# Two matmuls for three in a seven-product matmul scheme on one Trainium2 core

## The chip, the cores and the metric

The kernel runs on 1 core of one Trainium2 chip. The time is device microseconds of one execution of the whole program, as the median of the runs shown. TensorE (PE) multiplies, VectorE (DVE) and ScalarE (ACT) work on SBUF and PSUM, GpSimd (POOL) works on SBUF and issues the accumulating DMAs, SyncE (SP) issues the others.

## What is computed

A two-layer decoder trunk on 512 tokens of width 2048, all in float32. Cut to what matters here:

```python
def _stick_breaking_mixer(x, k, v, w_q, w_out):
    q, g = _split(x @ w_q, (ATTN_W, ATTN_W))
    ...
    return (o * jax.nn.silu(g)) @ w_out

def reference(x, p, positions, w_in_a, w_out_a, w_q_b, w_kv_b, w_out_b, ...):
    ...
        x = _layer_norm(DN_ALPHA * x + y, ln_g[i], ln_b[i])
        x = x + (p[i] @ w_ple[i]) * jax.nn.sigmoid(x @ w_ple_gate[i])
        if i == N_A_LAYERS - 1:
            kb, vb = _split(x @ w_kv_b, (ATTN_W, ATTN_W))
    ...
```

The change touches the projections `x @ w_kv_b` and `x @ w_q` of the second layer: keys, values, queries and gates of 16 heads, each a product of a 128-column block of weights (2048 x 128) with the 512 tokens.

## The kernel before

Everywhere in the kernel a float32 product is made of float32r parts: an operand is split into a high part (its float32r rounding, by ACT) and a low part (the rest, by DVE), and three matmuls are summed: high by high, low by high and high by low. The order of work is one list of `Chunk`s, each with the weights of one 128 x 1024 tile `raw`. `run` goes through the list; at chunk c `plan` has placed steps for later chunks: the split of the weights of chunk c + 2 into `wh` (ACT, L299) and `wl` (DVE, L300), loads six chunks ahead, and the weight sums below. Every engine works its instructions in the order in which they were issued, and the splits come ahead of what a chunk's own end issues.

**The seven products.** `quads` (L194) works off 30 pairs of weight blocks. For a pair, blocks c1 and c2 are cut into row halves, the 2048 x 512 input into four quarters, and seven products P1 to P7 of sums of these give both 128 x 512 results (a Strassen-Winograd scheme). A product has one 128 x 1024 weight tile and one table of 8 input tiles `f` from `F` ("A11", "S1" and so on). Each `f` is 128 x 512: its first 256 columns (`HALF`) are the high part of 256 columns of input, its last 256 the low part (`split_halves`, L105). `form` (L856) hands the two halves out, and `multiply` (L186) runs 8 times three matmuls of 256 columns into the first half of a PSUM bank (L192).

**Banks and ends.** Bank E takes P7 and then P4, bank B takes P2, and bank A takes P1, P6, P5 and P3 in turn; a product that follows in the same bank adds to it, so intermediate values must be read out before the next one starts there. After P7, P1 and P6 ACT copies 256 columns of the bank to SBUF (`after7`, `after1`, `after6`); after P2, P5 and P4 DVE adds a copy and a bank, 128 x 256 (`after2` L237, `after5` L241, `after4` L245); after P3 ACT copies (`after3` L251). Then `b_done` takes a result over: for keys and queries a split, for gates a sigmoid and a product.

**Weight sums.** The tile of P6 is the sum of those of P7 and P1, and the tile of P4 of those of P6 and P2 (DVE, L292). The tiles of P7 and P5 get c2's half added by an accumulating DMA from POOL's queue (`add_load`, L287): that of P5 lands on the tile of P1 after P1's splits and P6's sum have read it, two chunks before P1 begins.

**Order of the pairs.** A pair's list is P7, P1, P3 of the pair before, P6, P2, P4, P5; the first pair starts with P1, P7, and the last P3 stands alone at the end. Attention of the heads is woven in: `b_att` (score matmuls, then ACT sigmoids, POOL masks, DVE scans) after P2 and P4 of the pair that follows a pair with a key block (15 of the 30 pairs, the last one among them), `b_tail` after P1 and P6 of the next (after the last P3 for the last head), and `b_values` (transposes) after P5 of the pair that has a value block. After the last pair's products `us_ahead` splits eight tiles `u` for the output projection `mix_out`.

```python
                product(q, "P3", "S4", "A", False, True, after3, fresh=(1, q["c"][1]))
...
            product(q, "P6", "S2", "A", False, False, after6, grown=q["P7"], plus=q["P1"])
            product(q, "P2", "A12", "B", True, True, after2, fresh=(1, c1))
            product(q, "P4", "A22", "E", False, True, after4, grown=q["P6"], plus=q["P2"])
            product(q, "P5", "S1", "A", False, False, after5, add=(0, c2), grown=q["P1"])
        third(qs[-1])
```

Of the kernel before, what the change touches and what calls it, by code (L numbers as in the profile page):

```python
# [10 lines left out]
OP = mybir.AluOpType  # L11
# [5 lines left out]
KT = D // P  # L17
# [14 lines left out]
HALF = T // 2  # L32
# [41 lines left out]
class Kernel:  # L74
# [109 lines left out]
            self.chunks.append(Chunk(loads, mms))  # L184

    def multiply(self, ch, ps, xs, start, stop):  # L186
        nc = self.nc
        for j in range(KT // 2):
            wh, wl = (z[:, j * P:(j + 1) * P] for z in (ch.h, ch.l))
            xh, xl = xs(j)  # L190
            for n, (a, b) in enumerate(((wh, xh), (wl, xh), (wh, xl))):
                nc.tensor.matmul(ps[:, :HALF], a, b, start=start and j == 0 and n == 0,  # L192
                                 stop=stop and j == KT // 2 - 1 and n == 2, skip_group_check=True)

    def quads(self, sources, forms, done):

        nc = self.nc
        seq = []

        def product(q, name, form, acc, start, stop, after, fresh=None, add=None, grown=None, plus=None):  # L200
            def run(ch):
                if start:
                    q[acc] = self.ps("g")
                self.multiply(ch, q[acc], lambda j: forms(form, j), start, stop)
                after(q)
                ch.h = ch.l = None

            def rows(half, block):
                view, c = block
                return view[:, half::2, c:c + P]  # L210

            def loads(raw):
                nc.sync.dma_start(raw.rearrange("p (k c) -> p k c", k=8), rows(*fresh))

            ch = Chunk(loads if fresh else None, [])
            ch.product = run
            ch.grown = grown
            ch.add = rows(*add) if add else None
            ch.plus = plus
            q[name] = ch  # L220
            seq.append(ch)

        def after7(q):
            q.setdefault("s17", None) or q.__setitem__("s17", self.tt(s="s17"))
            nc.scalar.copy(q["s17"][:, HALF:], q["E"][:, :HALF])

        def after1(q):
            q.setdefault("s17", None) or q.__setitem__("s17", self.tt(s="s17"))
            nc.scalar.copy(q["s17"][:, :HALF], q["A"][:, :HALF])

        def after6(q):
            q["o2"] = self.tt(s="o2")
            nc.scalar.copy(q["o2"][:, :HALF], q["A"][:, :HALF])

        def after2(q):
            q["o1"] = self.tt(s="o1")
            nc.vector.tensor_tensor(q["o1"][:, :HALF], q["s17"][:, :HALF], q["B"][:, :HALF], op=OP.add)  # L237
            q["B"] = None

        def after5(q):  # L240
            nc.vector.tensor_tensor(q["o2"][:, HALF:], q["s17"][:, HALF:], q["A"][:, :HALF], op=OP.add)  # L241
            q["s17"] = None

        def after4(q):
            nc.vector.tensor_tensor(q["o1"][:, HALF:], q["o2"][:, :HALF], q["E"][:, :HALF], op=OP.add)  # L245
            q["E"] = None
            done(q["n"], 0, q["o1"])
            q["o1"] = None

        def after3(q):  # L250
            nc.scalar.copy(q["o2"][:, :HALF], q["A"][:, :HALF])  # L251
            q["A"] = None
            done(q["n"], 1, q["o2"])
            q["o2"] = None

        qs = [dict(n=n, c=c) for n, c in enumerate(sources)]
        for n, q in enumerate(qs):
            c1, c2 = q["c"]
            last = qs[n - 1] if n else None

            def third(q):
                product(q, "P3", "S4", "A", False, True, after3, fresh=(1, q["c"][1]))

            if not last:
                product(q, "P1", "A11", "A", True, False, after1, fresh=(0, c1))
            product(q, "P7", "S3", "E", True, False, after7, fresh=(1, c2), add=(0, c2))
            if last:
                product(q, "P1", "A11", "A", True, False, after1, fresh=(0, c1))
                third(last)
            product(q, "P6", "S2", "A", False, False, after6, grown=q["P7"], plus=q["P1"])  # L270
            product(q, "P2", "A12", "B", True, True, after2, fresh=(1, c1))
            product(q, "P4", "A22", "E", False, True, after4, grown=q["P6"], plus=q["P2"])
            product(q, "P5", "S1", "A", False, False, after5, add=(0, c2), grown=q["P1"])
        third(qs[-1])
        self.chunks += seq
        return qs
# [110 lines left out]
def _emit(k, x, p, positions, w_in, w_out_a, w_q, w_kv, w_out_b, ln_g, ln_b, w_ple, w_gate, freq, out):  # L387
    nc, const = k.nc, k.const
# [201 lines left out]
    xs = lambda m: xT[m]  # L590
# [252 lines left out]
    F = {}  # L843
# [11 lines left out]
        k.split_halves(f24, ((j, F["S2"]), (j, F["S4"])))  # L855

    def form(name, j):
        f = F[name][j]
        return f[:, :HALF], f[:, HALF:]

    def ln_apply(layer, ms):
        for m in ms:
# [203 lines left out]
    qs = k.quads([(where_b[a](ha), where_b[b](hb)) for a, ha, b, hb in plan_b], form, b_done)  # L1066
    for n, (a, ha, b, hb) in enumerate(plan_b):
        if a == "v":
            qs[n]["P5"].then(lambda h=ha: b_values(h))
        if a != "k":  # L1070
            continue
        qs[n + 1]["P2"].then(lambda h=ha: b_att(h, 0, 1))
# [4 lines left out]
    last = qs[-1]  # L1077
# [58 lines left out]
```

## Time and profile before

| what | value |
|---|---|
| median of 3 runs | 2148.35 us (2148.02 to 2149.95) |
| profiled execution, its own time | 2148.99 us |
| its span in the trace | 2147.3 us |
| PE busy | 2120.2 us, 99% of the span |
| PE weight loads busy | 1876.8 us, 87% |
| DVE busy | 1354.8 us, 63% |
| ACT busy | 967.9 us, 45% |
| POOL busy | 262.9 us, 12% |
| mean granted clock of PE | 0.996 |

The pairs of the seven-product scheme take 1056 to 1752 us of the span. A busy share tells how long an engine had an instruction in it; matmuls overlap each other, so what one costs is read from the distance of the starts of neighbours and not from its duration. A wait in the trace is idle time of an engine with the instruction that ended it. The profiled execution's own time is 0.64 us above the median, and 1.7 us above its span for what lies around it.

### The profile page before, as it was taken

What the parts mean: (1) busy time and instruction counts of PE and PEld (TensorE: products, weight loads), DVE (VectorE), ACT (ScalarE), POOL (GpSimd) and SP (SyncE); (2) the same over time, 40 slices, a digit from 0 to 9 for tenths busy, and PEclk for the clock granted to TensorE, in tenths of its full rate; (3) what the DMA queues carried; (4) which work ended last, traced back from release to release, by engine and by line L of the source; (5) the groups of instructions that cost most, each with busy time, mean ns of one, the idle gap of its engine ahead of it and who ended that gap; (6) DMA issues with size and microseconds to landing.
All of it is one profiled execution on the core that took longest, in us unless ns stands there. A gap on an engine that the chain in (4) does not pass through costs nothing.

```text
span 2147.3 us, 30976 instructions
## 1 busy us (share of the span) xinstructions
PE 2120.2 (99%) x12289; PEld 1876.8 (87%) x12289; DVE 1354.8 (63%) x2063; ACT 967.9 (45%) x1529; POOL 262.9 (12%) x287
## 2 busy tenths in 40 slices
PE   8999999999999999999999999999999989999999
PEld 7987888888888887888899999999999988887887
DVE  3576976566566547635778777777777765447432
ACT  3564345455453226423555455455555443226422
POOL 6111010000000100000022122121221111110000
PEclk9999999999999999999999999999999999999999
DMA  7332332222222232333567777778768863332341
GB/s 220 109 89 79 98 99 78 71 79 69 79 89 89 90 107 79 128 118 121 115 134 134 148 141 142 149 144 150 155 124 150 176 178 115 118 118 74 103 122 55
DMA packets 368800, 248.72 MB, mean 116 GB/s; under 512 B 13648, under 2 KB 354704, under 8 KB 368656
## 3 DMA queue, kind: packets, MB, share of 16 engines
q1 hardware_dynamic: 306256, 215.29, 34.9%
q0 software_dynamic: 62400, 31.46, 11.8%
q8 instruction: 96, 1.57, 0.3%
q14 instruction: 48, 0.39, 0.1%
HBM read 234.65 MB, written 12.06 MB: 115 GB/s over the span
## 4 chain that ended last, share of the span: by engine, by line
PE 92%; DVE 3%; issue 3%; ACT 1%; POOL 1%; DMA 0%; SPq 0%; POOLq 0%; DVEq 0%; ACTq 0%
PE g L192 25%; PE g L118 19%; PE g L119 19%; PE g L120 19%; PE s L611 2%; PE o L119 1%; PE o L120 1%; PE o L118 1%; PE s L118 1%; PE s L119 1%; PE s L120 1%; DVE wl L300 1%; PE s L545 1%; DVE z L866 1%; DVE z L865 0%
## 5 line engine op out<-in xcount | busy, mean ns | idle before, releaser
L300 DVE TENSOR_TENSOR wl<-raw,wh 128x1024 fp32r<-128x1024 f32 x452 | 555.8, 1234 | 389.7 <-ACT wh L299 386.4
L118 PE MATMUL g<-h,wh 128*128 128x512 f32 (+1 forms) x1808 | 704.4, 390 | 3.3 <-ACT h L102 3.3
L119 PE MATMUL g<-l,wh 128*128 128x512 f32 (+1 forms) x1808 | 698.9, 387 | 3.2 <-DVE l L103 3.2
L120 PE MATMUL g<-h,wl 128*128 128x512 f32 (+1 forms) x1808 | 698.5, 386 | 0.5 <-DVE wl L300 0.5
L192 PE MATMUL g<-f,wh 128*128 128x256 f32 x3360 | 621.6, 284 | 5.6 <-DVE o L241 5.6
L299 ACT CAST wh<-raw 128x1024 fp32r<-128x1024 f32 x452 | 473.0, 1051 | 335.6 <-PE g L119 223.7
L192 PEld LDWEIGHTS g<-f,wh 128*128 128x128 f32 x3360 | 530.5, 192 | 6.6 <-issue 5.8
L192 PE MATMUL g<-f,wl 128*128 128x256 f32 x1680 | 476.6, 284 | 1.9 <-DVE wl L300 1.9
L118 PEld LDWEIGHTS g<-h,wh 128*128 128x128 f32 x1808 | 340.1, 188 | 73.9 <-ACT h L102 4.8
L119 PEld LDWEIGHTS g<-l,wh 128*128 128x128 f32 x1808 | 340.4, 188 | 69.3 <-DVE l L103 4.8
L120 PEld LDWEIGHTS g<-h,wl 128*128 128x128 f32 x1808 | 340.2, 188 | 67.1 <-DVE wl L300 1.0
L192 PEld LDWEIGHTS g<-f,wl 128*128 128x128 f32 x1680 | 323.2, 192 | 3.5 <-DVE wl L300 2.7
L287 POOL DMA_DIRECT2D raw<-in_w_q_b_dram x60 | 94.4, 1894 | 571.9 <-issue 244.4
L103 DVE TENSOR_TENSOR l<-s,h 128x512 fp32r<-128x512 f32 (+1 forms) x128 | 73.0, 618 | 47.2 <-ACT h L102 47.2
L488 POOL TENSOR_TENSOR rb<-rb,sin 128x512 f32<-128x512 f32 (+2 forms) x29 | 36.0, 1241 | 475.3 <-ACT rb L486 320.2
L669 ACT ACTIVATE pr<-pr,s 128x128 f32<-128x128 f32 (+1 forms) x64 | 36.1, 563 | 126.1 <-DVE s L668 125.8
L102 ACT CAST h<-s 128x512 fp32r<-128x512 f32 (+1 forms) x128 | 61.1, 540 | 62.1 <-PE s L448 33.2
L815 POOL TENSOR_TENSOR a<-a,sq 128x512 f32<-128x512 f32 x30 | 40.3, 1343 | 342.1 <-ACT sq L813 341.9
L292 DVE TENSOR_TENSOR raw<-raw,raw 128x1024 f32<-128x1024 f32 x60 | 73.1, 1219 | 0.0
L684 DVE TENSOR_TENSOR_SCAN r<-keep,zeros 128x127 f32<-128x127 f32 (+1 forms) x64 | 54.4, 849 | 13.0 <-POOL keep L681 13.0
L489 DVE TENSOR_TENSOR ra<-ra,cos 128x512 f32<-128x512 f32 (+2 forms) x29 | 32.8, 1131 | 37.6 <-ACT ra L487 37.6
L813 ACT ACTIVATE sq<-z 128x512 f32<-128x512 f32 x30 | 19.0, 634 | 81.6 <-DVE z L806 81.6
(183 smaller groups left out, 1956.0 us busy)
## 6 DMA issues: line engine op xcount, KB each, us to landing
raw<-in_w_in_a_dram SPq DMA_DIRECT2D x132, 256.0 KB, 3.3
raw<-in_w_ple_gate_dram SPq DMA_DIRECT2D x64, 512.0 KB, 3.7
raw<-in_w_kv_b_dram SPq DMA_DIRECT2D x64, 512.0 KB, 6.4
raw<-in_w_q_b_dram SPq DMA_DIRECT2D x64, 512.0 KB, 6.9
raw<-in_w_q_b_dram POOLq DMA_DIRECT2D x60, 512.0 KB, 10.3
raw<-in_w_in_a_dram SPq DMA_DIRECT2D x32, 512.0 KB, 4.0
raw<-in_w_out_a_dram SPq DMA_DIRECT2D x32, 512.0 KB, 3.5
raw<-in_w_out_b_dram SPq DMA_DIRECT2D x32, 512.0 KB, 3.6
```

The lines of the kernel that those rows point to most:

```text
L102: nc.scalar.copy(h[:, lo:w], src[:, lo:w])
L103: nc.vector.tensor_tensor(l[:, lo:w], src[:, lo:w], h.bitcast(F32)[:, lo:w], op=OP.subtract)
L118: nc.tensor.matmul(out, ah, bh, start=start, stop=False)
L119: nc.tensor.matmul(out, ah, bl, start=False, stop=False)
L120: nc.tensor.matmul(out, al, bh, start=False, stop=stop)
L192: nc.tensor.matmul(ps[:, :HALF], a, b, start=start and j == 0 and n == 0, stop=stop and j == KT // 2 - 1 and n == 2, skip_group_check=True)
L287: self.nc.gpsimd.dma_start(ch.raw.rearrange("p (k c) -> p k c", k=8), ch.add, accum_op=OP.add)
L292: self.nc.vector.tensor_tensor(ch.raw, ch.raw, ch.plus.raw, op=OP.add)
L299: nc.scalar.copy(ch.h, ch.raw)
L300: nc.vector.tensor_tensor(ch.l, ch.raw, ch.h.bitcast(F32), op=OP.subtract)
L611: nc.tensor.transpose(banks[b][:, off + (i - j) * P:off + (i - j + 1) * P], a["p"][i][:, j * P:(j + 1) * P], ident)
L684: nc.vector.tensor_tensor_scan(r[:, 0:n - 1][:, ::-1], keep[:, 1:n][:, ::-1], zeros.to_broadcast([P, n - 1]), 1.0, op0=OP.mult, op1=OP.add)
```

## The change

In `multiply` the high weights meet a whole `f` tile, high and low half, in one matmul of 512 columns that fills the bank; the low weights still meet the high half in one of 256 columns. The two halves of a bank must now be added at some point. ACT's copies after P7, P1 and P6 (`snapshot`) take 512 columns into a tile each; after P2, P4 and P5 DVE adds copy and bank over 512 columns and then the two halves of the sum (`joined`); after P3 ACT copies the second half of the bank and DVE adds the first. In the last pair P5 comes right after P6, ahead of P2 and P4, and its value block's transposes move to its P3.

```diff
     def multiply(self, ch, ps, xs, start, stop):
...
-            xh, xl = xs(j)
-            for n, (a, b) in enumerate(((wh, xh), (wl, xh), (wh, xl))):
-                nc.tensor.matmul(ps[:, :HALF], a, b, start=start and j == 0 and n == 0,
-                                 stop=stop and j == KT // 2 - 1 and n == 2, skip_group_check=True)
+            x = xs(j)
+            last = stop and j == KT // 2 - 1
+            nc.tensor.matmul(ps, wh, x, start=start and j == 0, stop=last, skip_group_check=True)
+            nc.tensor.matmul(ps[:, :HALF], wl, x[:, :HALF], start=False, stop=last, skip_group_check=True)
...
+        def snapshot(q, name, bank):
+            q[name] = self.tt(s=name)
+            nc.scalar.copy(q[name], q[bank])
+
+        def joined(q, name, bank, out):
+            t = q.pop(name)
+            nc.vector.tensor_tensor(t, t, q[bank], op=OP.add)
+            nc.vector.tensor_tensor(out, t[:, :HALF], t[:, HALF:], op=OP.add)
+
         def after7(q):
-            q.setdefault("s17", None) or q.__setitem__("s17", self.tt(s="s17"))
-            nc.scalar.copy(q["s17"][:, HALF:], q["E"][:, :HALF])
+            snapshot(q, "s7", "E")
...
         def after6(q):
-            q["o2"] = self.tt(s="o2")
-            nc.scalar.copy(q["o2"][:, :HALF], q["A"][:, :HALF])
+            snapshot(q, "s2", "A")
...
         def after5(q):
-            nc.vector.tensor_tensor(q["o2"][:, HALF:], q["s17"][:, HALF:], q["A"][:, :HALF], op=OP.add)
-            q["s17"] = None
+            q["o2"] = self.tt(s="o2")
+            joined(q, "s7", "A", q["o2"][:, HALF:])
...
         def after3(q):
-            nc.scalar.copy(q["o2"][:, :HALF], q["A"][:, :HALF])
+            o = q["o2"][:, :HALF]
+            nc.scalar.copy(o, q["A"][:, HALF:])
+            nc.vector.tensor_tensor(o, o, q["A"][:, :HALF], op=OP.add)
...
             product(q, "P6", "S2", "A", False, False, after6, grown=q["P7"], plus=q["P1"])
+
+            def fifth():
+                product(q, "P5", "S1", "A", False, False, after5, add=(0, c2), grown=q["P1"])
+
+            if n == len(qs) - 1:
+                fifth()
             product(q, "P2", "A12", "B", True, True, after2, fresh=(1, c1))
             product(q, "P4", "A22", "E", False, True, after4, grown=q["P6"], plus=q["P2"])
-            product(q, "P5", "S1", "A", False, False, after5, add=(0, c2), grown=q["P1"])
+            if n < len(qs) - 1:
+                fifth()
         third(qs[-1])
...
     def form(name, j):
-        f = F[name][j]
-        return f[:, :HALF], f[:, HALF:]
+        return F[name][j]
...
-            qs[n]["P5"].then(lambda h=ha: b_values(h))
+            qs[n]["P5" if n + 1 < len(qs) else "P3"].then(lambda h=ha: b_values(h))
```

How the order of the instructions moves is shown at two places. The first is DVE in the twelfth pair (which has attention after P2 and P4), from ahead of the end of P4 to that of P5. `o1` and `o2` are the pair's results, `s17`, `s1`, `s2` and `s7` the copies, `g` the banks, `keep`, `beta` and `r` the attention's. Before:

```order
L300 TENSOR_TENSOR wl_2178_12138<-raw_2148_11917,wh_2177_12137 128x1024
L245 TENSOR_TENSOR o1_2168_12103<-o2_2164_12072,g_2151_11948 128x256
L683 MEMSET r_2183_12174 128x1
L684 SCALAR_TENSOR_TENSOR r_2183_12174<-keep_2181_12172,zeros_84 128x383
L686 TENSOR_TENSOR beta_2182_12173<-beta_2182_12173,r_2183_12174 128x384
L683 MEMSET r_2187_12190 128x1
L684 SCALAR_TENSOR_TENSOR r_2187_12190<-keep_2185_12188,zeros_84 128x511
L686 TENSOR_TENSOR beta_2186_12189<-beta_2186_12189,r_2187_12190 128x512
L300 TENSOR_TENSOR wl_2189_12201<-raw_2158_12011,wh_2188_12200 128x1024
L292 TENSOR_TENSOR raw_2148_11917<-raw_2148_11917,raw_2158_12011 128x1024
L241 TENSOR_TENSOR o2_2164_12072<-s17_2152_11973,g_2155_11979 128x256
```

The same stretch in the changed kernel:

```order
L316 TENSOR_TENSOR wl_2201_11558<-raw_2169_11380,wh_2200_11557 128x1024
L230 TENSOR_TENSOR s2_2187_11499<-s2_2187_11499,g_2173_11405 128x512
L231 TENSOR_TENSOR o1_2191_11522<-s2_2187_11499 128x256
L699 MEMSET r_2206_11587 128x1
L700 SCALAR_TENSOR_TENSOR r_2206_11587<-keep_2204_11585,zeros_84 128x383
L702 TENSOR_TENSOR beta_2205_11586<-beta_2205_11586,r_2206_11587 128x384
L699 MEMSET r_2210_11603 128x1
L700 SCALAR_TENSOR_TENSOR r_2210_11603<-keep_2208_11601,zeros_84 128x511
L702 TENSOR_TENSOR beta_2209_11602<-beta_2209_11602,r_2210_11603 128x512
L316 TENSOR_TENSOR wl_2212_11614<-raw_2181_11453,wh_2211_11613 128x1024
L308 TENSOR_TENSOR raw_2169_11380<-raw_2169_11380,raw_2181_11453 128x1024
L230 TENSOR_TENSOR s7_2174_11422<-s7_2174_11422,g_2177_11428 128x512
```

Nothing changes places; the ends of P2, P4 and P5 have two instructions for one, the first of 512 columns, and the scans and the `wl` splits of the next products stand behind them in the queue.

The second place is ACT in the last pair, from behind the copy that follows P1. `wh` are the splits of weights, here of P2, P4 and P5 before and of P5, P2 and P4 in the changed kernel; the raw tile 2884 (2941 in the changed kernel) is the one on which P5's accumulating DMA lands. Before:

```order
L299 CAST wh_2919_17131<-raw_2898_16990 128x1024
L251 COPY o2_2889_16938<-g_2872_16821 128x256
L1024 ACTIVATE h_2922_17163<-o2_2889_16938 128x512
L299 CAST wh_2924_17167<-raw_2862_16750 128x1024
L233 COPY o2_2927_17197<-g_2914_17097 128x256
L299 CAST wh_2932_17207<-raw_2884_16878 128x1024
L677 ACTIVATE keep_2938_17244<-s_2937_17240 128x128
```

In the changed kernel:

```order
L315 CAST wh_2978_15673<-raw_2941_15470 128x1024
L259 COPY o2_2960_15606<-g_2928_15420 128x256
L1039 ACTIVATE h_2981_15697<-o2_2960_15606 128x512
L315 CAST wh_2983_15701<-raw_2959_15588 128x1024
L226 COPY s2_2986_15724<-g_2972_15646 128x512
L315 CAST wh_2991_15734<-raw_2917_15363 128x1024
```

The split of P5's weights, which before stood behind the copy after P6, now stands five places further up, ahead of the copy after the previous pair's P3, of the split of P2's weights and of the copy after P6.

## Rows read from the trace of the kernel before

**Rows 1.** The page's part 1 (engine, busy us, share of the span, instructions).

```profile
PE 2120.2 (99%) x12289; PEld 1876.8 (87%) x12289; DVE 1354.8 (63%) x2063; ACT 967.9 (45%) x1529; POOL 262.9 (12%) x287
```

**Rows 2.** Windows: us, then busy us of PE, PEld, DVE, ACT, POOL, PEclk, DMA.

```profile
1056.00:1752.00 696.00, 688.48 (x5612) 683.34 (x5611) 514.56 (x680) 356.37 (x570) 142.96 (x187) 1.00 0.75 148
1746.70:1752.20 5.50, 5.49 (x26) 5.50 (x27) 4.00 (x6) 0.00 (x0) 0.00 (x0) 0.50 0.66 206
```

**Rows 3.** Timeline of PE in a product: start us, us, engine, line, instruction.

```profile
1299.73 0.28 PE L192 MATMUL g<-f,wl 128*128 128x256 f32 x1
...
1309.81 0.28 PE L192 MATMUL g<-f,wl 128*128 128x256 f32 x1
```

**Rows 4.** Timeline of PE, 512-column matmuls of a gate projection.

```profile
900.26 0.39 PE L118 MATMUL g<-h,wh 128*128 128x512 f32 x1
...
903.66 0.39 PE L118 MATMUL g<-h,wh 128*128 128x512 f32 x1
```

**Rows 5.** Timeline of PE, 512-column matmuls of an attention head.

```profile
1342.97 0.40 PE L118 MATMUL o<-h,h 128*128 128x512 f32 x1
...
1343.67 0.34 PE L118 MATMUL o<-h,h 128*128 128x384 f32 x1
```

**Rows 6.** Groups of instructions by line and shape: busy us, mean ns, idle before.

```profile
L625 DVE TENSOR_TENSOR u<-o,th 128x512 f32<-128x512 f32 x16 | 11.1, 692 | 30.9 <-PE o L120 30.9
L876 ACT COPY ple<-g 128x512 f32<-128x512 f32 x32 | 17.7, 587 | 4.6 <-PE g L120 4.5
```

**Rows 7.** Timeline of DVE, two adds of which the second needs the first.

```profile
967.05 0.69 DVE L938 TENSOR_TENSOR sg<-sg,ple 128x512 f32<-128x512 f32 x1 [1.26 <-ACT sg L937]
967.78 0.69 DVE L939 TENSOR_TENSOR sg<-sg,z 128x512 f32<-128x512 f32 x1
```

**Rows 8.** Timeline of DVE from P2 of the twelfth pair on.

```profile
1323.50 0.48 DVE L684 TENSOR_TENSOR_SCAN r<-keep,zeros 128x127 f32<-128x127 f32 x1 [0.59 <-POOL keep L681]
...
1326.66 0.42 DVE L245 TENSOR_TENSOR o<-o,g 128x256 f32<-128x256 f32 x1
...
1327.46 0.96 DVE L684 TENSOR_TENSOR_SCAN r<-keep,zeros 128x383 f32<-128x383 f32 x1 [0.38 <-POOL keep L681]
...
1331.10 1.22 DVE L300 TENSOR_TENSOR wl<-raw,wh 128x1024 fp32r<-128x1024 f32 x1
...
1333.37 0.42 DVE L241 TENSOR_TENSOR o<-s,g 128x256 f32<-128x256 f32 x1
...
1334.30 2.35 DVE L300 TENSOR_TENSOR wl<-raw,wh 128x1024 fp32r<-128x1024 f32 x2
```

**Rows 9.** Timeline of PE: first use of `wl` by P1, and by P3.

```profile
1333.37 0.28 PE L192 MATMUL g<-f,wl 128*128 128x256 f32 x1
...
1337.34 0.28 PE L192 MATMUL g<-f,wl 128*128 128x256 f32 x1
```

**Rows 10.** Waits in the window 1056:1752: us in total, times, longest us.

```profile
PE g L192 <- DVE wl L300: 1.9, 4, 0.5
```

**Rows 11.** Timeline of POOL and ACT in the last pair.

```profile
1720.86 1.55 POOL L287 DMA_DIRECT2D raw<-in_w_q_b_dram  x1 [18.69 <-issue]
...
1727.71 0.63 ACT L1024 ACTIVATE h<-o 128x512 fp32r<-128x512 f32 x1
...
1730.18 0.37 ACT L233 COPY o<-g 128x256 f32<-128x256 f32 x1 [0.90 <-PE g L192]
1733.06 1.05 ACT L299 CAST wh<-raw 128x1024 fp32r<-128x1024 f32 x1 [2.50 <-DMA raw<-in_w_q_b_dram]
```

**Rows 12.** Timeline of DVE and PE in the last pair.

```profile
1734.14 1.23 DVE L300 TENSOR_TENSOR wl<-raw,wh 128x1024 fp32r<-128x1024 f32 x1 [3.60 <-ACT wh L299]
...
1746.71 0.55 PE L192 MATMUL g<-f,wh 128*128 128x256 f32 x1 [5.59 <-DVE o L241]
...
1751.97 1.37 PE L611 MATMUL s<-ident,beta 128*128 128x128 f32 x10
```

**Rows 13.** The accumulating DMAs' time from issue to landing, by tile.

```profile
DMA to landing us min/median/max: 6.8/10.3/13.6
```

More of the change, by code (lines that the diff above doesn't have):

```diff
@@ L221, in product @@
             seq.append(ch)
+        def snapshot(q, name, bank):
[5 more added lines that the diff above has]
+            nc.vector.tensor_tensor(out, t[:, :HALF], t[:, HALF:], op=OP.add)
         def after7(q):
-            q.setdefault("s17", None) or q.__setitem__("s17", self.tt(s="s17"))
-            nc.scalar.copy(q["s17"][:, HALF:], q["E"][:, :HALF])
+            snapshot(q, "s7", "E")
         def after1(q):
-            q.setdefault("s17", None) or q.__setitem__("s17", self.tt(s="s17"))
-            nc.scalar.copy(q["s17"][:, :HALF], q["A"][:, :HALF])
+            snapshot(q, "s1", "A")
         def after6(q):
-            q["o2"] = self.tt(s="o2")
-            nc.scalar.copy(q["o2"][:, :HALF], q["A"][:, :HALF])
+            snapshot(q, "s2", "A")
         def after2(q):
             q["o1"] = self.tt(s="o1")
-            nc.vector.tensor_tensor(q["o1"][:, :HALF], q["s17"][:, :HALF], q["B"][:, :HALF], op=OP.add)
+            joined(q, "s1", "B", q["o1"][:, :HALF])
             q["B"] = None
         def after5(q):
-            nc.vector.tensor_tensor(q["o2"][:, HALF:], q["s17"][:, HALF:], q["A"][:, :HALF], op=OP.add)
-            q["s17"] = None
+            q["o2"] = self.tt(s="o2")
+            joined(q, "s7", "A", q["o2"][:, HALF:])
         def after4(q):
-            nc.vector.tensor_tensor(q["o1"][:, HALF:], q["o2"][:, :HALF], q["E"][:, :HALF], op=OP.add)
+            joined(q, "s2", "E", q["o1"][:, HALF:])
             q["E"] = None
```

## The prediction, written before the changed kernel ran

> **What bounds the kernel.** I read the busy shares first: PE is busy for 99% of the span [rows 1], so an engine beside it matters only where PE waits for it. The window of the seven-product pairs says the same: in 696 us PE is busy for 688 and DVE for 515, 74%, at a granted clock of 1.00 [rows 2]. The waits there name two PE stalls: 1.9 us in four waits for a `wl` split [rows 10] and one of 5.6 us ahead of the last P3 [rows 12]. So the stretch is a stream of matmuls at full clock, and the question is what one costs there, and then whether DVE stays ahead of a faster stream.
>
> A matmul's busy time overlaps its neighbours'; what counts is the distance of starts. From 1299.73 to 1309.81 stand 28 triples [rows 3]: 10.08 us / 28 = 360 ns a triple, 120 ns a matmul of 256 columns. In the gate projection, where `wh` is also the loaded weight and a tile of 512 columns streams, 15 matmuls take 3.40 us [rows 4]: 226.7 ns each. The second 256 columns therefore cost 106.7 ns (2.4 GHz, the granted clock), and each matmul has 13.3 ns besides that do not depend on its width.
>
> **Term 1, the matmuls.** A position j had three matmuls, 3 x 120 = 360 ns; it now has one of 512 and one of 256 columns, 226.7 + 120 = 346.7 ns. The columns are the same 768; one fixed share is gone. 30 pairs x 7 products x 8 positions = 1680 positions x 13.3 ns = **22.4 us less**. The bound from the other side is an attention head's 512-column rows: three take 0.70 us, 233 ns each [rows 5], which leaves 360 - 353 = 6.7 ns, 11.2 us. I take the gate's rows: the same operands (weights `wh`, a 512-column tile, a bank summed over many matmuls), while the head's are three in a row per tile. On the fixed share the Trainium skill, in "TensorE: Matmul & The Clock Gate", section "Wait — 56ns, not 53.3ns?", states about 2.5 ns per warm matmul. By that figure the term would be 1680 x 2.5 = 4.2 us; the rows above, where neighbours load other weights each time, show 13.3, and the sum goes by them.
>
> **Term 2, DVE's joins.** An end was one add of 256 columns, 0.42 us [rows 8]. Now an add of 512 columns with one operand in PSUM comes first, 0.69 us [rows 6], and the add of 256 that needs its result can start 0.73 us after it [rows 7]. So **each join is 0.73 us longer**, three a pair, and P3's end has an add of 0.42 us more: 2.6 us a pair, 78 us in all, on 515 of what becomes about 680 us: 87% busy. That is no bound in itself, and the joins hide beside PE as long as the next `wl` is ready in time. ACT's copies grow from 0.37 to 0.59 us [rows 6, 11]; ACT is busy for 356 of 696 us [rows 2] and its splits are chunks ahead, so I cost them at nothing outside the last pair.
>
> Where is the cover thin? In the 15 pairs with attention, DVE runs from the end of P2 to the next pair's P1 almost without a break [rows 8]. 11 of 15 look like the twelfth pair. P1's `wl` ends at 1331.10 + 1.22 = 1332.32 and is used at 1333.37 [rows 8, 9]: 1.05 us to spare. P2's longer join eats 0.59 us of idle time ahead of the first scan and passes on 0.14; P4's eats 0.38 and passes on 0.35 [rows 8]: `wl` is 0.49 later. P4, P5 and P7 are 3 x 0.107 = 0.32 faster, and the first use of `wl` in a product now comes 0.11 later: PE arrives 0.21 sooner. 1.05 - 0.49 - 0.21 = 0.35 us left. P3's `wl`, the first of the two at 1334.30, ends near 1335.5 and is used at 1337.34: 1.8 us, less 0.49 + 0.73 (P5's join) and 0.32: 0.3 left. **No stall there, but little room.** P3 also waits in bank A for the first add of P5's join; that began at 1333.37, so it is done 2 us early. In the four pairs where PE already waits for P1's `wl` [rows 10], P4's join goes in full onto that path, because what follows it (ACT's takeover of the result) waits for it: 0.73 + 0.21 = 0.94 us each, **3.8 us more**. The bounds are 0 (all absorbed) and 6.7 (P2's join passes through as well).
>
> **Term 3, the last pair.** Before, P3 waited 5.6 us for DVE behind P5, and the clock fell: 0.50 (1.2 GHz) from 1746.7 to 1752.2 [rows 2], so that P3 took 1751.97 - 1746.71 = 5.26 us [rows 12] for 24 x 0.12 = 2.88: 2.4 us lost. Together 8.0 us, and the reorder takes this wait away, since P2 and P4 now stand between P5 and P3. **What is late next is P5 itself.** Its weights are the tile on which the accumulating DMA lands, issued at 1720.86 and ready at 1733.06, when ACT had waited 2.5 us for it [rows 11]: 12.2 us, where such DMAs take 6.8 to 13.6 [rows 13]. P5's place is now that of P2, right after P6, which ended near 1730.1 [rows 11]. The issue itself doesn't move up: it waits for P6's weight sum, which stands on DVE behind P4's join of the pair before, 0.73 later: the tile is ready at 1733.8. ACT, in order, stands in front of it, and behind it stand the copy after the other pair's P3, its takeover, P2's weights and the copy after P6, for which P5 must wait, since it adds into the same bank. In durations: `wh` to 1734.85; DVE's `wl` starts 1.08 behind the start of `wh` [rows 11, 12] and ends at 1736.1; P3's new add 0.42, to 1736.5; takeover 0.63, to 1737.15; `wh` of P2 1.05, to 1738.2; the copy 0.59, to 1738.8. P6 ends 5 x 0.107 earlier than before, near 1729.6. PE stands still for 9.2 us, and I charge the same 2.4 us for the clock. After P4 the last head's scans now have one product of cover: DVE needs 1.15 us for the join and 3.6 for the scans and masks [rows 8], PE has 2.8 us of P3 and the scores meanwhile; I take 0.8 us of waiting, between 0 and 2. 9.2 + 2.4 + 0.8 - 8.0 = **4.4 us more**. The bounds: with 6.8 us for the landing the stall shrinks by 5.4 and, if the clock then holds, by 2.4 more: -3.4; with 13.6 us it is +5.8.
>
> **Sum.** -22.4 + 3.8 + 4.4 = -14.2 us on the profiled execution's 2148.99, 2134.8; that execution is 0.64 above the median, so the median is forecast at **2134.2 us**. With the small bounds of terms 2 and 3 the case lies between 2130 and 2139.
>
> **Rivals.**
> *The DMA lands early.* For it: the median is 10.3 us, not 12.2. Against: the DMA queues are busiest here, and the one measured landing at this place is 12.2. With 6.8 us: -22.4 + 3.8 - 3.4 = -22.0, 2126.3 us. The Trainium skill's "DMA: Bandwidth & Descriptors", section "Anatomy of one DMA — SWDGE (gpsimd) path", gives 2.0 us plus the bytes at 436 GB/s: an estimate of 3.2 us for these 512 KB. By that estimate P5 would wait for the copy alone (0.9 + 0.8 - 8.0 us in term 3) and the kernel would take about 2123.5 us; the trace disagrees, its shortest landing being 6.8 us [rows 13].
>
> *The 512-column matmul is dearer.* If it costs what the head's do, 233 ns, the sum is -11.2 + 3.8 + 4.4 = -3.0, 2145.4 us, within 0.2%. Should it cost two of 256, 240 ns, nothing is gained: 2156.6 us. The sign turns where the saving is 8.2 us, at 235 ns.
>
> *DVE becomes the bound, and the kernel slower.* The place is the run of DVE from P2's end to P3's `wl` in the 15 attention pairs, the price every 0.1 us that a join costs more than I take: two joins lie ahead of P3's `wl`, 0.2 us a pair. The 0.3 us of room is gone at 0.15 us a join; the gain is gone when a pair loses 14.2 / 15 = 0.95 us, at 0.6 us a join. At 1 us more it is 15 x 1.7 = 25 us: 2160 us. For it: 87% busy, and room of 0.3 us in 11 pairs. Against: both adds have measured rows of their own shape, and after P3 DVE has idle time in which a delay runs out.
>
> **Chances.** A measurement of this kernel tells about 0.2%, 4.3 us, from no change. Forecast 0.70; early landing 0.13: both faster, 0.83. The head's price for 512 columns 0.07, and DVE eating most of the gain 0.04: within 0.2%, 0.11. DVE as the bound 0.04 and 240 ns 0.02: slower, 0.06. The range takes in the first three cases, 2126 to 2147.
>
> **What would show it.** PE's timeline: starts alternating by 227 and 120 ns, a product in 2.77 us. Waits of PE on `wl`: some 5 to 6 us in four waits at P1, none to speak of elsewhere; if instead some 15 short waits stand at P1 or P3, DVE is the bound. Last pair: one idle of some 9 us between P6 and P5, ended by ACT's copy L226, `wh` ahead of it having waited for the DMA, and P5 at half clock; no wait ahead of P3. The prediction is wrong if the 512s start 233 ns or more apart, or if P5 starts within 4 us of P6.

## The result and the profile after

The changed kernel takes **2158.51 us** (2157.48 to 2161.76, 4 runs) where the kernel before takes 2148.41 beside it: ratio 1.0052, 95% interval 1.004 to 1.0063. The prediction was 2134.2 us and faster; the kernel is 10.1 us slower. The profiled execution took 2161.76 us, 3.3 more than the median, so its losses are a little larger than a typical run's.

The page's part 1 of the changed kernel, as [rows 1]:

```profile
span 2160.0 us, 27792 instructions
...
PE 2115.3 (98%) x10609; PEld 1789.8 (83%) x10609; DVE 1421.2 (66%) x2183; ACT 982.7 (45%) x1529; POOL 260.1 (12%) x287
```

DVE has 66.4 us more work, where 78 were reckoned. The windows answer to [rows 2]: the stage of the pairs, then two stretches at 1.2 GHz (PEclk 0.50), one around the last pair's P5, one at the start of the output projection, where before there was none.

```profile
1056.00:1752.00 696.00, 677.86 (x3908) 592.81 (x3907) 570.36 (x783) 366.25 (x562) 138.06 (x184) 0.99 0.75 146
1733.00:1743.20 10.20, 5.22 (x16) 4.46 (x17) 5.83 (x6) 6.49 (x10) 0.00 (x0) 0.50 0.42 138
1757.00:1767.20 10.20, 5.65 (x17) 4.42 (x18) 7.97 (x12) 3.39 (x6) 0.00 (x0) 0.50 0.31 105
```

PE idles 18 us of the stage's 696 instead of 7.5. **The stream itself is faster**, as the timeline of PE in a product shows (as [rows 3]):

```profile
1266.03 0.40 PE L193 MATMUL g<-f,wh 128*128 128x512 f32 x1
1266.27 0.28 PE L194 MATMUL g<-f,wl 128*128 128x256 f32 x1
1266.38 0.40 PE L193 MATMUL g<-f,wh 128*128 128x512 f32 x1
...
1268.73 0.28 PE L194 MATMUL g<-f,wl 128*128 128x256 f32 x1
1268.85 0.40 PE L193 MATMUL g<-f,wh 128*128 128x512 f32 x1
```

From 1266.03 to 1268.85 are eight positions: 352.5 ns each, some 235 and 117 in turn, where the old triple takes 360. Over the whole stage of this trace, the positions without a wait and at full clock take 351 ns in the mean, 9 ns less than before. **The time goes into waits of PE**, here from 1040 us to 1765 (engine and line that waits, what for: us in total, times, longest), where before only 1.9 us for `wl` [rows 10] and the wait of [rows 12] stood:

```profile
PE g L194 <- DVE wl L316: 11.0, 11, 2.1
PE g L193 <- ACT s L226: 6.9, 1, 6.9
PE s L627 <- DVE l L103: 4.5, 1, 4.5
PE s L627 <- DVE beta L702: 1.6, 1, 1.6
PE s L627 <- DVE r L699: 0.6, 1, 0.6
```

The first row is P1's `wl`: four waits of 1.4 to 2.1 us in the early pairs whose P4 result DVE must also split, and shorter ones in the later pairs. In the first ones the clock falls too (PE's timeline, two positions of P1, 0.64 us each):

```profile
1145.73 0.45 PE L194 MATMUL g<-f,wl 128*128 128x256 f32 x1 [2.09 <-DVE wl L316]
1145.97 0.63 PE L193 MATMUL g<-f,wh 128*128 128x512 f32 x1
1146.40 0.41 PE L194 MATMUL g<-f,wl 128*128 128x256 f32 x1
1146.62 0.63 PE L193 MATMUL g<-f,wh 128*128 128x512 f32 x1
```

The last pair, as [rows 11, 12]: P5's weights land 10.5 us after POOL's issue, and P5 starts 6.92 us late, at half clock (0.64 us a position).

```profile
1722.70 1.55 POOL L303 DMA_DIRECT2D raw<-in_w_q_b_dram  x1 [18.05 <-issue]
...
1733.21 1.04 ACT L315 CAST wh<-raw 128x1024 fp32r<-128x1024 f32 x1 [7.19 <-DMA raw<-in_w_q_b_dram]
...
1737.34 0.58 ACT L226 COPY s<-g 128x512 f32<-128x512 f32 x1
...
1737.97 0.79 PE L193 MATMUL g<-f,wh 128*128 128x512 f32 x1 [6.92 <-ACT s L226]
```

And the part that was not foreseen, behind the last P3 (PE, then DVE, then ACT):

```profile
1753.64 0.60 PE L1050 MATMUL s<-ident,o 128*128 128x128 f32 x4
...
1757.01 1.33 PE L627 MATMUL s<-ident,beta 128*128 128x128 f32 x5 [1.61 <-DVE beta L702]
1762.88 0.69 PE L627 MATMUL s<-ident,beta 128*128 128x128 f32 x2 [4.53 <-DVE l L103]
...
1756.87 2.49 DVE L103 TENSOR_TENSOR l<-u,h 128x512 fp32r<-128x512 f32 x4
1759.28 1.22 DVE L316 TENSOR_TENSOR wl<-raw,wh 128x1024 fp32r<-128x1024 f32 x1
1760.42 0.41 DVE L260 TENSOR_TENSOR o<-o,g 128x256 f32<-128x256 f32 x1
...
1762.14 0.68 DVE L103 TENSOR_TENSOR l<-s,h 128x512 fp32r<-128x512 f32 x1
...
1760.87 0.63 ACT L1032 ACTIVATE sg<-o 128x512 f32<-128x512 f32 x1 [5.42 <-DVE o L260]
```

The transposes of `b_values` (L1050) now come after the last P3 and take one of three PSUM banks "s". The last head's transposes (L627) need three, so they wait until DVE has split `b_values`' bank, at 1762.14: behind the scans, the takeover of four tiles `u`, a `wl`, and P3's new add, for which ACT and everything behind it wait 5.42 us. From the end of the last P3 to the end of the span are 406.2 us, before 395.1: of the 12.7 us by which this span is longer, **11.1 stand there**. The stage of the pairs gains some 15 us at 9 ns for 1680 positions, loses all of it to the waits and the lower clock, and is 3.4 us longer than before (699.6 against 696.2, first P1 to the end of the last P3).

### The profile page after: what moved, and what is told of

Read it like the earlier page. It is cut to its first block, busy times and chain, and to the rows that moved or that the text cites. A ratio compares the mean times of both kernels' runs of the same rounds, so it can differ in the third digit from the quotient of the medians.

```text
span 2160.0 us, 27792 instructions
## 1 busy us (share of the span) xinstructions
PE 2115.3 (98%) x10609; PEld 1789.8 (83%) x10609; DVE 1421.2 (66%) x2183; ACT 982.7 (45%) x1529; POOL 260.1 (12%) x287
## 4 chain that ended last, share of the span: by engine, by line
PE 71%; issue 12%; DVE 7%; DMA 7%; ACT 2%; POOL 1%; SPq 0%; DVEq 0%; POOLq 0%; ACTq 0%
PE g L118 19%; PE g L119 19%; PE g L120 19%; DMA raw<-in_w_q_b_dram 6%; PE g L193 5%; PE g L194 3%; DVE wl L316 2%; PE s L627 2%; DVE r L700 1%; ACT wh L315 1%; DVE z L881 1%; PE s L561 1%; DVE z L880 1%; PE o L120 1%; PE o L119 1%
## 5 line engine op out<-in xcount | busy, mean ns | idle before, releaser
L193 PE MATMUL g<-f,wh 128*128 128x512 f32 x1680 | 603.1, 401 | 6.9 <-ACT s L226 6.9
L194 PE MATMUL g<-f,wl 128*128 128x256 f32 x1680 | 475.4, 283 | 11.1 <-DVE wl L316 11.0
L193 PEld LDWEIGHTS g<-f,wh 128*128 128x128 f32 x1680 | 318.8, 190 | 80.3 <-ACT s L226 7.3
L194 PEld LDWEIGHTS g<-f,wl 128*128 128x128 f32 x1680 | 320.4, 191 | 17.0 <-DVE wl L316 15.5
L226 ACT COPY s<-g 128x512 f32<-128x512 f32 x90 | 52.5, 584 | 76.6 <-PE g L194 76.5
L230 DVE TENSOR_TENSOR s<-s,g 128x512 f32<-128x512 f32 x90 | 61.5, 683 | 18.3 <-PE g L194 18.1
```

Source lines behind the costliest of these rows:

```text
L193: nc.tensor.matmul(ps, wh, x, start=start and j == 0, stop=last, skip_group_check=True)
L194: nc.tensor.matmul(ps[:, :HALF], wl, x[:, :HALF], start=False, stop=last, skip_group_check=True)
L230: nc.vector.tensor_tensor(t, t, q[bank], op=OP.add)
```

## Experiments

Each median is over 4 to 11 runs, the ratio against the kernel before, run beside it (2147.8 to 2148.6 us). "Old order" means the last pair in its order before.

| run | us | ratio, 95% interval |
|---|---|---|
| old_order | 2145.94 | 0.999 (0.9981 to 0.9999) |
| order_only | 2155.05 | 1.0031 (1.0019 to 1.0044) |
| joins_only | 2153.35 | 1.002 (1.0011 to 1.0029) |
| no_joins | 2134.59 | 0.9932 (0.992 to 0.9945) |
| after_tail | 2155.93 | 1.0045 (1.0032 to 1.0059) |
| last_snap | 2142.86 | 0.998 (0.9971 to 0.9989) |
| last_free | 2146.10 | 0.9993 (0.9984 to 1.0002) |
| pool_sums | 2211.18 | 1.0298 (1.0284 to 1.0312) |
| both | 2207.46 | 1.0272 (1.0258 to 1.0286) |
| wl_first | 2195.30 | 1.0216 (1.0199 to 1.0233) |
| best | 2192.48 | 1.0203 (1.0189 to 1.0217) |
| before_fix | 2152.59 | 1.0023 (1.0013 to 1.0032) |
| split_first | 2145.23 | 0.9986 (0.9977 to 0.9995) |
| split_best | 2136.74 | 0.9946 (0.9933 to 0.9958) |
| split_before | 2138.01 | 0.9954 (0.9942 to 0.9967) |
| mixed | 2139.80 | 0.9962 (0.9949 to 0.9974) |
| mixed_inv | 2146.02 | 0.999 (0.9981 to 0.9999) |
| **mixed_best** | **2130.45** | **0.9918 (0.9905 to 0.9932)** |

### The three parts of the change, one at a time

**old_order**, the changed kernel without the reorder:

```diff
-            if n == len(qs) - 1:
-                fifth()
             product(q, "P2", ...)
             product(q, "P4", ...)
-            if n < len(qs) - 1:
-                fifth()
+            fifth()
```

> The changed kernel with the last pair in its old order (P6, P2, P4, P5, P3), all else as changed. Theory A, the reorder costs at the end: after the last P3 the changed kernel needs 11.2 us more than before, and its stall between P6 and P5 with the half clock behind it about 12 us against 8.0 before; so about 13 to 15 us come back, 2158.5 becomes about 2145 (2142 to 2149), with no half-clock stretch after the last P3. Rival, the joins cost at the end: P3's new add on DVE stands behind the last head's work whatever the order, so that only the 4 us at P5 come back: about 2154.

**order_only**, the kernel before with the reorder alone (the same lines the other way):

> The kernel before with the last pair reordered alone (256-column products, old joins). Theory A: the stall between P6 and P5 of about 7 us and a half-clock stretch stand here too, and the last head's scans reach PE late after P3, so 2148.4 becomes about 2160 (2155 to 2163). Rival, the joins make the end late: only the 4 us at P5 show, about 2152, and the end after P3 stays near 395 us.

**joins_only**, old order, new joins, old width:

```diff
-            nc.tensor.matmul(ps, wh, x, ...)
+            nc.tensor.matmul(ps[:, :HALF], wh, x[:, :HALF], start=first, ...)
             nc.tensor.matmul(ps[:, :HALF], wl, x[:, :HALF], ...)
+            nc.tensor.matmul(ps[:, HALF:], wh, x[:, HALF:], start=first, ...)
```

The third matmul's own start flag opens the bank a second time, which leaves the first position's part of the lower half out of P1, P7 and P2; number and size of the instructions are those meant. (The Trainium skill, "PSUM — Partial Sum Buffer", section "The four PSUM rules", says that a start clears the marks of a whole bank, whichever part is written; no row here shows it.)

> Old order, the new joins, but each position still three matmuls of 256 columns (the third goes to the upper half of the bank). Positions stay at 360 ns. Theory A, the joins' length alone makes DVE late: the stalls at P1 rise from 2.6 us to some 7 us plus lost clock, about 2155 (2151 to 2159). Rival, they are only late for a faster stream: with 360 ns positions the stalls stay below 4 us and the time within 2 us of before, about 2150.

**no_joins**, old order, new matmuls, ends as before (`after1` to `after7` and `after3` of the kernel before):

> Old order, the new matmuls (512 and 256 columns), but the ends as before: the copies and adds take the lower half of each bank alone, so the upper halves (input low parts times weight high parts) are left out of the result. Theory A, the stream gains 7 to 10 ns a position over 1680 positions: 12 to 17 us, and nothing of it is lost at P1: about 2133 (2130 to 2138), positions of 350 to 353 ns. Rival, the 512-column matmul brings nothing in the stream (position 358 ns or more): 2146 or more. My prediction's 13.3 ns would give 2126.

The waits of PE, 1040 to 1765 us, of order_only, then joins_only, no_joins and old_order:

```profile
PE g L192 <- ACT o L233: 6.4, 1, 6.4
PE s L621 <- DVE l L103: 4.0, 1, 4.0
PE g L192 <- DVE wl L310: 1.9, 4, 0.5
...
```

```profile
PE g L195 <- DVE wl L315: 6.5, 4, 2.1
PE g L194 <- DVE s L232: 5.9, 1, 5.9
```

```profile
PE g L193 <- DVE o L242: 6.8, 1, 6.8
PE g L194 <- DVE wl L305: 2.1, 4, 0.6
```

```profile
PE g L194 <- DVE wl L313: 12.0, 12, 2.6
PE g L193 <- DVE s L230: 6.5, 1, 6.5
```

Step by step the time goes from 2148.56 to 2134.59 with the matmuls (-14.0), to 2145.94 with the joins (+11.4), to 2158.51 with the reorder (+12.6). A part's price depends on what it is added to: the joins cost 4.8 us at the old 360 ns (joins_only), the reorder 6.5 us alone (order_only).

The joins' 11.4 us are for the most part P1's waits (12.0 against 2.1 us in the rows; old_order's profiled execution is 2.7 us above its median). Of the 12.0 us, 7.5 are the four early waits and 4.6 the eight later ones (rounded). joins_only has the four early ones alone, so the later eight need the faster stream as well.

order_only's stage is 0.6 us longer than before, and its end behind P3 takes 402.3 us instead of 395.1, with the same wait for a bank. In the changed kernel, with joins and faster stream, that end takes 3.9 us more. old_order, joins_only and no_joins came out as their theory A said. order_only lies at the lower edge of its range, but the rival's end near 395 us did not come.

**after_tail** tests the reading of the end: the changed kernel, with the takeover of `u` moved.

```diff
-    last["P4"].then(lambda: us_ahead(0))
...
-    last["P3"].then(lambda: (F.clear(), b_tail(HEADS - 1, 0)))
+    last["P3"].then(lambda: (F.clear(), b_tail(HEADS - 1, 0), us_ahead(0)))
```

> The changed kernel, its new order kept, with the first takeover of u moved from P4's end to behind the last head's transposes. Theory, the wait of 4.9 us after the last P3 is for a PSUM bank that is freed by a split on VectorE behind that takeover and P3's new add: about 2 us come back, 2158.5 becomes 2156 (2153.5 to 2157.5), and ScalarE's wait of 5.4 us for P3's add falls to about 3. Rival, the wait is for the scans alone: the time stays at 2158 or above.

The trace agrees with the theory: the wait for the bank is 2.7 us instead of 4.5, and the end behind P3 takes 404.7 us instead of 406.2. ACT's wait for P3's add is 4.29 us, less of a fall than the 3 expected, as the scans stay ahead of it. The median, 2155.93 us, is the one expected, but its interval (1.0032 to 1.0059) overlaps that of the changed kernel (1.004 to 1.0063), so the time alone doesn't show the gain.

### VectorE: the order of its queue, or its work

**pool_sums** moves both weight sums (`add_plus`) from DVE to POOL:

```diff
-        self.nc.vector.tensor_tensor(ch.raw, ch.raw, ch.plus.raw, op=OP.add)
+        self.nc.gpsimd.tensor_tensor(ch.raw, ch.raw, ch.plus.raw, op=OP.add)
```

> As old_order, but the two weight sums of a pair (a tile of 1024 columns each, 1.22 us on VectorE) run on GpSimd. Theory, VectorE's length of work ahead of P1's wl is what makes PE wait: 2.4 us a pair leave VectorE, about what the joins added, so the stalls at P1 fall from 13 us to about 3 and the time from 2145.9 to about 2135 (2132 to 2140). Rival, the landing of the accumulating DMAs is the cause: behind a slower sum on GpSimd they are issued later still, ScalarE waits longer for raw, and the time stays at 2146 or rises.

65 us slower than old_order. A sum takes POOL 2457 ns in the mean, its DMA issues and masks stand behind it, and PE's waits for `wl` grow to 46.8 us in 17 times. DVE, which was to be relieved, became slower itself: its scans take 1216 ns in the mean, 845 in old_order. So this run can't tell the two theories apart; the traces further down can.

**wl_first** issues the next chunk's whole step ahead of the second half of the scans (`self.ahead(c + 1)` between the product of P4 and its `after`):

> As old_order, but in the 15 attention pairs the split of P1's weights and the weight sum behind it are issued ahead of the second half of the attention's scans, not behind them (no work is removed). Theory, PE waits at P1 because VectorE takes P4's longer join and the scans before wl: wl comes 3 to 4 us earlier, the 12 or 13 waits at P1 fall from 13 us to under 2 and the clock holds there: 2145.9 becomes about 2133.5 (2131 to 2137). Rival, it is the sum of VectorE's work: the waits only move to the scans' results (the transposes after P1, P3's wl), 2142 or more.

Missed by 60 us, and by my edit: the step also holds POOL's accumulating DMA, and POOL takes its queue in order. Its timeline:

```profile
1348.40 1.56 POOL L301 DMA_DIRECT2D raw<-in_w_q_b_dram  x1 [8.15 <-ACT wh L313]
1349.32 0.96 POOL L697 TENSOR_SCALAR_AFFINE_SELECT keep<-keep 128x128 f32<-128x128 f32 x1
```

The masks start 3.4 us after ACT's last sigmoid (1345.9), and the scans and transposes are late with them. **split_first** moves the split alone (`early` is set for P4 of the pairs with scans):

```diff
+            if ch.early:
+                _, n, split = self.steps[c + 1].pop(0)
+                split(n)
             if ch.after:
                 ch.after()
```

> As old_order, but in the 15 attention pairs the split of P1's weights alone (ScalarE's copy and VectorE's subtraction) is issued ahead of the second half of the attention's scans; the weight sum and the accumulating DMAs keep their place. In wl_first GpSimd's queue held a DMA issue, 8.2 us late, ahead of the masks that the scans need, which hid what the split's place does. Theory, the waits at P1 come from VectorE's order: wl is 3.4 us earlier, the scans 1.2 us later, which the product P1 covers; the waits fall from 13 us to under 2: about 2133.5 (2131 to 2137). Rival, VectorE's sum of work in these pairs is what bounds them: the waits come back at the transposes behind P1 or at P3, 2142 or more.

The rival was right. P1 no longer waits, but P3's `wl` and the transposes behind P1 do (PE's waits; the first row holds the 6.7 us of the last pair):

```profile
PE g L194 <- DVE s L231: 8.0, 3, 6.7
PE g L195 <- DVE wl L314: 7.9, 13, 1.0
PE s L629 <- DVE l L104: 0.7, 2, 0.6
```

Some 10 us of waiting are left of 12: the place of one split doesn't free the stretch. **mixed** and **mixed_inv** put the joins in one half of the pairs each: `multiply`, `snapshot`, `joined` and `after3` take the new form if the pair's `wide` is set, otherwise that of before.

```diff
-        qs = [dict(n=n, c=c) for n, c in enumerate(sources)]
+        qs = [dict(n=n, c=c, wide=n not in narrow) for n, c in enumerate(sources)]
```

`narrow` are the 16 pairs with scans, the last one among them (the 15 given ahead of the prediction are one too few).

> Old order; the 14 pairs in which no scans of the attention run have the new 512-column products and joins, the 16 pairs with scans have the old three products of 256 columns and the old ends. Theory, the joins cost PE time only where VectorE has scans too: half the stream's gain of some 15 us stays and no new wait arises, 2147.9 becomes about 2141 (2139 to 2144), waits at P1 as before (2.6 us). Rival, the loss is spread over all pairs: half the gain and half the loss, about 2147.

> Old order; the other way round: new products and joins in the 16 pairs with scans alone. Theory: some 8 us of gain in the stream and the whole loss of old_order, 10 us more waiting at P1 and 1 to 2 us of clock: about 2151 (2148 to 2154). Rival, the loss is spread: about 2147.

mixed fits: 2139.80 us, 1.7 us of waits for `wl`. mixed_inv fits neither theory: 2146.02 us is near the rival's 2147, but it has the four early waits alone (5.9 us in two rows of two), and no later one. The two gains, 8.4 and 2.2 us, together exceed old_order's 2.6 us by far. So the later waits need the new form in neighbouring pairs of both kinds: lateness is carried from pair to pair.

What carries it stands in the traces: ACT, DVE and PE in the twelfth pair and at the next P1, first old_order, then mixed_inv. The first `wl` of each is that of the next pair's P7, the second that of its P1.

```profile
1327.99 1.05 ACT L312 CAST wh<-raw 128x1024 fp32r<-128x1024 f32 x1 [2.86 <-DMA raw<-in_w_q_b_dram]
1329.08 1.23 DVE L313 TENSOR_TENSOR wl<-raw,wh 128x1024 fp32r<-128x1024 f32 x1 [1.89 <-ACT wh L312]
...
1334.88 1.22 DVE L313 TENSOR_TENSOR wl<-raw,wh 128x1024 fp32r<-128x1024 f32 x1
1336.15 0.39 PE L194 MATMUL g<-f,wl 128*128 128x256 f32 x1 [1.12 <-DVE wl L313]
```

```profile
1325.97 1.22 DVE L326 TENSOR_TENSOR wl<-raw,wh 128x1024 fp32r<-128x1024 f32 x1
...
1331.79 1.22 DVE L326 TENSOR_TENSOR wl<-raw,wh 128x1024 fp32r<-128x1024 f32 x1
1333.48 0.28 PE L199 MATMUL g<-f,wl 128*128 128x256 f32 x1
```

From the first `wl` to the second DVE needs 5.8 us in both (the `wl`, P4's join and two scans). In mixed_inv that leaves 0.47 us to spare at P1, near the 0.35 that the prediction reckoned. In old_order DVE doesn't run short of time here: it stands idle for 1.89 us, since ACT's `wh` waits 2.86 us for P7's accumulating DMA. All eight late waits look like this: ACT waits 1.7 to 2.9 us for that DMA and DVE idles 0.6 to 1.9 us. In the same eight pairs ACT waits at most 0.4 us in mixed_inv and 1.4 in joins_only, and P1 doesn't wait; in no_joins it waits up to 1.45, but DVE's ends are short. So the late waits take both, the longer joins and the late DMA. In split_first too, ACT waits 1.7 to 2.7 us for the DMA ahead of each of the nine late waits at P3.

The DMA comes late in old_order for two reasons of about 1 us each: in the mean of these eight pairs it is issued 14.5 us ahead of P4's end (15.5 in mixed_inv), and takes 13.4 us to land (12.2). POOL issues it only when DVE has made the weight sum, which stands behind the joins of the pair before; that would close the loop. Why it also takes longer to land is open, and no run moves the issue alone. The four early waits are another matter: they stand in mixed_inv as well, with the DMA in time.

### The last pair, and a faster version

**last_snap** (old order): after the last P5 ACT copies bank A, and the join reads the copy, so that P3 needn't wait for DVE.

```diff
+            if q["n"] == len(sources) - 1:
+                snapshot(q, "s5", "A")
+                joined(q, "s7", "s5", q["o2"][:, HALF:])
```

> As old_order, but in the last pair ScalarE copies bank A after P5 and the join reads the copy, so that P3 need not wait for the join on VectorE. Theory, P3's wait of 6.7 us is VectorE's queue alone: it falls to under 2 us (ScalarE is free about 1 us after P5's end), and some 2.5 us come back as a wait of the last head's transposes for a PSUM bank: 2145.9 becomes about 2141 (2138 to 2144). Rival, the wait only moves: the last head's transposes take all of it, about 2145.

As expected: P3 waits 1.5 us, the transposes 2.2, and no half clock stands there. The time is 3.1 us under old_order's, with overlapping intervals of the ratio. **last_free** adds the takeovers of `u` behind P5's join, with POOL subtracting:

> As last_snap, and the eight takeovers of u ahead of the output projection stand after P5's join, their subtraction on GpSimd in place of VectorE. Theory, VectorE's queue is what is late in the last pair: 5 us less on it, the bank for the transposes is free near P3's end, PE waits under 2 us in all there, and the half-clock stretch goes: about 2138 (2135 to 2141). Rival, GpSimd's subtractions are late for the output projection: a wait of several us behind P3, 2142 or more.

A miss, at the rival's time but with another wait. While POOL subtracts, DVE is slower (timelines of POOL and DVE):

```profile
1738.13 13.46 POOL L103 TENSOR_TENSOR l<-u,h 128x512 fp32r<-128x512 f32 x8 [2.83 <-ACT h L102]
...
1738.37 1.62 DVE L704 TENSOR_TENSOR beta<-beta,r 128x512 f32<-128x512 f32 x1
1739.90 2.30 DVE L318 TENSOR_TENSOR wl<-raw,wh 128x1024 fp32r<-128x1024 f32 x1
1742.13 1.75 DVE L230 TENSOR_TENSOR s<-s,s 128x512 f32<-128x512 f32 x1
1743.91 1.37 DVE L231 TENSOR_TENSOR o<-s 128x256 f32<-128x256 f32 x1
1745.20 0.68 DVE L103 TENSOR_TENSOR l<-s,h 128x512 fp32r<-128x512 f32 x1
```

The last row is the split of `b_values`' bank, for which the transposes wait 4.9 us.

**both** (pool_sums with last_free) falls with the same cause:

> pool_sums and last_free together. If the two losses are separate, their gains add: about 2145.9 - 11 - 8 = 2127 (2124 to 2133), below the kernel before by 1 percent. Rival, with the stalls at P1 gone PE arrives earlier in the last pair and finds the same late queue: 2134 or more.

**best** (wl_first, last_snap, and the takeovers moved, on DVE) and **before_fix** (the same on the kernel before) carry wl_first's fault, and neither comes near its forecast; in best's last pair PE waits only 0.2 us ahead of P3, so that part is kept.

```diff
-    last["P4"].then(lambda: us_ahead(0))
-    last["P5"].then(lambda: us_ahead(1))
-    last["P3"].then(lambda: (F.clear(), b_tail(HEADS - 1, 0)))
+    last["P5"].then(lambda: us_ahead(0))
+    last["P3"].then(lambda: (F.clear(), b_tail(HEADS - 1, 0), us_ahead(1)))
```

> wl_first with last_snap's copy in the last pair, and the first takeover of u moved behind P5's join, the second behind P3. Theory: the gains add, 13 us and 3 us, and 2 us more where the last head's transposes no longer wait for a bank behind the takeover: about 2129 (2126 to 2133). Rival, the takeovers are now late for the output projection: 2133 or more.

> The same three moves on the kernel before (256-column products, short joins). Its waits at P1 are 2.6 us and its wait in the last pair 5.6 us with 2.4 us of clock, so it gains about 6 us: 2148 becomes 2142 (2139 to 2145). With best at 2129 the products of 512 columns are then worth 13 us, the saving of the stream in full. Rival, with VectorE's queue in order the change brings nothing: both within 4 us.

**split_best** and **split_before** have split_first's edit instead:

> split_first with ScalarE's copy of bank A after the last P5, the first takeover of u behind P5's join and the second behind the last head's transposes. In best, with the same end, PE waited 0.4 us ahead of the last P3 and 1.1 us behind it. Theory: 6.5 us of waiting and the half-clock stretch of 6.8 us go, 2 to 3 us come back behind P3: about 2127 (2124 to 2131). Rival: 2133 or more.

> The same moves on the kernel before. Its waits at P1 are 2.6 us, its wait in the last pair 5.6 us with 2.4 us of clock: about 2141 (2138 to 2145). If split_best is at 2127, the 512-column products are worth 13 to 14 us once VectorE's order is right, and the loss of the changed kernel lies in the order of work and not in the products. Rival: both within 5 us.

split_before came as forecast: it has no wait of PE in these 700 us and gains 9.9 us without any 512-column product. For split_best the rival was right: it gains 9.2 us on old_order, still waits (7.1 us for `wl`, 1.3 for transposes), and is only 1.3 us ahead of split_before, with overlapping intervals. Where the order is put right for both, the change as a whole is worth about nothing. The 8.4 us of waits are the larger part of the some 15 us that the stream saves; where the rest goes is open. **mixed_best** is split_best with the new products in the 14 pairs without scans:

> mixed with the moves of split_best. Theory: split_before's order has no wait of PE left, and the 14 pairs save 6 to 7 us on it: about 2131.5 (2129 to 2134), the fastest of all. Rival, the faster half of the stream uncovers VectorE again in the pairs with scans: 2136 or more.

As forecast, the fastest of all, 0.8% under the kernel before, with 0.9 us of waits left in the stage:

```profile
PE g L200 <- DVE wl L332: 0.9, 2, 0.6
```

## Why the prediction was wrong

Forecast were 14.2 us less, measured 10.1 more. The 24.3 us between come in about equal parts from the three terms: 8.4, 7.6 and 8.2.

- **Term 1, the matmuls: right in kind, a third too large.** 22.4 us were reckoned, 14.0 measured (no_joins), some 15 if the last pair's wait, 1.2 us longer there, is taken off: 9 ns a position. The step that failed is the choice of the gate's rows [rows 4] over the head's [rows 5]: a 512-column matmul between those of 256 takes some 233 to 235 ns here, and the 256-column one 117 instead of 120.
- **Term 2, the joins: the step that failed is ACT's splits, of which the prediction says "its splits are chunks ahead, so I cost them at nothing outside the last pair".** 3.8 us were reckoned, 11.4 measured. The joins' price was right (0.68 and 0.43 us for the two adds), and so was the sum of DVE's work that left P1 some room (0.35 us reckoned, 0.47 in mixed_inv). But in eight of the 11 pairs ACT's split waits 1.7 to 2.9 us for an accumulating DMA, and P1's `wl` is late with it: 4.6 us for which nothing was reckoned. That the DMA is issued behind DVE's joins was seen in term 3, for the last pair alone. DVE did have the idle time in which a delay was to run out; it spent it waiting for that split. The four early waits were reckoned at 5.7 us in all (1.9 + 3.8); they are 5.9 in mixed_inv, where the DMA is in time, and 7.2 to 7.5 where it isn't. The half clock behind some of them (3.4 us each, three times in the changed kernel's profiled run) had no term.
- **Term 3, the reorder: the step that failed is the end, "0.8 us of waiting, between 0 and 2".** 4.4 us more were reckoned, 12.6 measured. The wait at P5 was 6.9 us, reckoned 9.2, mainly since the DMA landed in 10.5 us and not 12.2; the chain named (DMA, ACT's copy, half clock, nothing ahead of P3) was right. Behind P3 I counted the scans and forgot that `b_values` had moved there too, with a bank that only DVE frees, that the takeover of `u` stands ahead of that on DVE, and that P3's new add stands in between with ACT behind it. This end is 11.1 us longer in the profiled run, with a second half-clock stretch. Without the reorder the sign turns: old_order is faster than before, if barely.
- **The rivals.** "DVE becomes the bound" named the right side, a kernel slower than before, and by chance nearly the time (2160 us), at 0.04. Its mechanism, dearer joins, was not what happened, and the place it named, the attention pairs, has only part of the loss: 11.1 us stand behind the last P3. The dearer 512-column matmul, at 0.07, was right about the rows.

## What to carry to other kernels

A matmul stream that gets faster moves every deadline behind it: before an edit that also adds work to the engine that feeds it, look not only whether each single piece is in time, but also which transfers that engine's work releases, and follow a delay through them to the next round. An idle engine does not absorb a delay if its idle time is a wait for what it released too late. Where a step is moved to the end of a stage, list what it holds (banks, queue places) and who frees them. The change paid where the feeding engine was idle (the pairs without scans), which is found by turning it on in one kind of stretch at a time.

## What was not expected of the hardware

- **Tensor operations on POOL slow DVE.** Beside POOL's eight subtractions (1716 ns each) DVE's `wl` took 2.30 us instead of 1.22, and the join's SBUF add 1.37 instead of 0.43. The Trainium skill, "SBUF — State Buffer", section "🔬 SBUF: two separate sides", says that the two engines share a port pair, which an operation of either holds to its end, on VectorE's side among others one with two SBUF inputs. These rows agree: the four DVE operations that took about twice as long or more have two SBUF inputs, and the split at 1745.20, which reads `s` from PSUM, kept its 0.68 us.
- **The clock.** In the changed kernel's profile three of the four early waits (1.80, 2.09 and 1.91 us) were followed by 3.4 us at 1.2 GHz, the one of 1.37 was not; in old_order only the one of 2.57 was, and one of 2.15 was not. The same kind of wait does not always cost the clock.
